# A hybrid encoder trunk: order of work by estimated times, and merged products in the units with stationary weights

## The chip, the cores and the metric

The kernel runs on one core of one Trainium2 chip. The metric is the device time of one execution in microseconds (us). PE is TensorE, PEld its weight loads, DVE VectorE, ACT ScalarE, POOL GpSimd and SP SyncE, which here only issues transfers.

## What is computed

Two layers work on 256 tokens of width 2048 (float32). Each normalises the stream, multiplies it by one wide input matrix, and feeds four branches: A, an S5 state-space layer (forward and backward scans, gelu, a gate product w_glu); B, a gated DeltaNet over six heads with a short convolution; C, grouped-query attention with eight heads; M, cross-attention into 256 memory tokens. Each branch result is multiplied by silu(z), lifted by its rows of w_branch, weighted by a sigmoid gate and summed; one output matrix and the residual end the layer. Cut to what matters:

```
h = rmsnorm(x) @ w_in            # u za | dq dk dv da db zb | aq ak av zc | mq zm | gate
yA, yB, yC, yM = s5(u), deltanet(dq, dk, dv, da, db), attention(aq, ak, av), memory(mq, mem)
merged = sum(sigmoid(gate_i) * ((y_i * silu(z_i)) @ w_branch_i) for i in "ABCM")
x = x + merged @ w_out
```

## The kernel before, in words

**The weight stream.** All weight matrices are packed into chunks of 128x1024 (512 KB). `layer_units` lists the units of a layer in the order of `ORDER`, and `layer` (from L1404) goes through them. `pump_raw` (L372) loads a chunk through SP's queue into one of three buffers. `pump_split` turns it into two parts, hi = rounded copy (ACT) and lo = raw - hi (DVE), each in three buffers; `hi` and `lo` are issued two chunks ahead (`AHEAD`). Activations (xT, memT, y, sy, mT) lie in two parts as well, side by side: `[128, 4, 2, 256]`.

**The products.** `run_unit` (its product is L418) multiplies a unit's chunks into one of two accumulators of two PSUM banks, `acc`. There are three kinds of units. N units (gates, branch and output products and some others) keep activations stationary and stream 512 weight columns. T units (u, km, mq, the DeltaNet projections dqkv, the four z and glu) and the one D unit per layer (dab) keep a tile of weights stationary and stream 256 tokens; a T unit of 16 row tiles has four chunks. Per weight tile there are three products: hi by activation hi, hi by activation lo, and, later in the chunk, lo by activation hi. All three go into columns 0 to 255 of a bank:

```
405  c = kk * u.cols
...
418  nc.tensor.matmul(o, w, x, start=start, stop=stop)
```

The line numbers are those of the profile. Line L240 is a helper through which all other instructions of PE, ACT and DVE are recorded, so these rows are told apart by their tiles: `bank` is one of four PSUM banks of the branches, `scr` one of 13 scratch tiles.

**Evacuation.** After a unit, `evac_<name>` reads `acc[:, :, 0:256]` (T) or all of it (N). For dqkv, ACT makes the centre tap of the convolution and DVE adds the four others, all from PSUM; for the z units, ACT takes tanh and DVE multiplies.

**The order around it.** Every branch is a set of generators, here called fibers. After every half chunk of products (6 or 12 matmuls) a tick passes. A fiber yields the number of ticks it wants to let pass; of those that are due, the one with the lowest rank goes on, as long as a count of issued work on DVE and ACT stays under a limit (`Meter`, `LIMIT`). S5 has rank 5, the last, in layer 0 and 3 in layer 1. All instructions thus stand in a fixed order on each engine's queue, written at build time; an instruction at the head of a queue that waits for a semaphore holds up those behind it.

```
while all(self.load[e] < self.LIMIT[e] for e in self.load):
    f = next((f for f in self.fibers if f[0] <= self.tick_no), None)
    if f is None:
        break
    self.rank = f[2]
    f[0] = self.tick_no + next(f[1])
```

**Steps that the prediction speaks of.** In S5, `chunk_sums` runs as three fibers over twelve blocks: two loads of 256 KB (L1253), 4 ticks, then TensorE multiplies the block directly (`bank<-scr,s5u`). `outputs` runs as two fibers: two loads of Wd (L1302, L1303) and two of Cd (L1305), 6 ticks, an addition on DVE and two copies on ACT, 2 ticks, the product, a copy, 2 ticks, a transposition, 1 tick, a copy. Then eight transfers write the result (L1338), one reads it back in another layout (L1343, `s5y`), and the gelu makes `sy`, the activations of glu. Before the first unit of each z the stream waits for the branch's result, before the products of M for attention's normed queries (`cqT`).

Of the kernel before, what the change touches and what calls it, by code (L numbers as in the profile page):

```python
# [2 lines left out]

# [10 lines left out]
AP = bass.AP  # L14
# [45 lines left out]
class Unit:  # L60
    def __init__(self, kind, name, src, nk, layer, idx=0, br=None):
        self.kind, self.name, self.src, self.nk = kind, name, src, nk
        self.layer, self.idx, self.br = layer, idx, br
# [11 lines left out]
def layer_units(layer):  # L75
    """The weight stream of one layer, in the order in which the tensor engine takes it."""
# [47 lines left out]
def dqkv_tile(j):  # L124
    """The j-th 128-column tile of the DeltaNet projections, head by head."""
# [4 lines left out]
def pack_weights(inp):  # L130
    """All weight matrices as the stream of [128, 1024] chunks that the kernel reads."""
# [23 lines left out]
def pack_small(inp):  # L155
    """Gains, biases and the like, per layer, one value or row per partition."""
# [20 lines left out]
def pack_s5(inp):  # L177
    """Per layer and partition (direction, state): a, log step, b and c; and d as diagonal blocks."""
# [12 lines left out]
def shape_consts():  # L191
    """Constants that follow from the shapes: identity, rotary angles, masks of the two directions."""
# [20 lines left out]
class Bank:  # L213
    """A set of equal tiles handed out and taken back in program order."""

    def __init__(self, tiles):
        self.free = list(tiles)

    def put(self, *tiles):
        self.free += tiles  # L220


class Meter:
# [5 lines left out]
    def __init__(self, eng, load, names, per, fixed):  # L229
        self._e, self._load, self._names, self._per, self._fixed = eng, load, names, per, fixed  # L230

    def __getattr__(self, name):
        f = getattr(self._e, name)

        def call(*args, **kw):
            o = kw.get("in_", kw.get("out", args[0] if args else None))
            if o is not None and name != "dma_start":
                for e in self._names:
                    self._load[e] += self._fixed + self._per * o.free_size()
            return f(*args, **kw)  # L240
        return call


class Builder:
    # microseconds of each engine per tick, and the backlogs between which the branches' work goes on
    DRAIN = {"V": 1.1, "S": 1}
    LIMIT = {"V": 2.125, "S": 2}
    FLOOR = {"V": 0.7, "S": 0.8}
    # memory attention, DeltaNet, attention and S5 by layer, and the preparation of S5
    RANK = ((3, 2, 4, 5), (5, 2, 4, 3))  # L250
    PREP_RANK = (3.5, 2.5)
    # ticks between the work of another engine and the tensor engine's use of it
# [3 lines left out]
    def __init__(self, ctx, tc, a, out):  # L256
        self.tc, self.nc, self.a, self.out = tc, tc.nc, a, out
        self.ready, self.count, self.acts = set(), {}, {}
        self.fibers, self.deferred, self.tick_no, self.rank = [], [], 0, 0
        self.load = {"V": 0.0, "S": 0.0}  # L260
        self.at = 0
        self.V = Meter(tc.nc.vector, self.load, "V", 1.04e-3, 0.06)
        self.S = Meter(tc.nc.scalar, self.load, "S", 0.84e-3, 0.19)
        self.PE = Meter(tc.nc.tensor, self.load, "VS", -0.6e-3, -0.02)
# [1362 lines left out]
```

## Time and profile before

| | |
|---|---|
| runs | 2330.08, 2333.71, 2336.09 us |
| median | 2333.71 us |
| profiled execution, span | 2329.0 us |
| mean granted TensorE clock | 0.990 of full speed |
| DMA | 523.39 MB, 225 GB/s on average |

The span is from the first to the last instruction of one profiled execution, whose own time as a run is not given beside it; the runs lie 1 to 7 us above it. Busy time on PE is an upper figure, since its products overlap in the rows.

### The profile page before, as it was taken

The numbers are of one execution on the slowest core, as the hardware profiler recorded it, in microseconds if no ns is written. First come the engines' busy times: TensorE is split into PE (matmuls) and PEld (weight loads), VectorE is DVE, ScalarE is ACT, GpSimd is POOL, SyncE is SP. The second block draws the span as 40 slices with busy tenths as digits, with TensorE's granted clock in tenths as the row PEclk, the third lists the DMA queues.
The fourth block names the chain that finished last, engine by engine and source line by source line (L and its number), as shares of the span: only waits on it lengthen the run. The fifth ranks groups of instructions, "written<-read, shape, count | busy, mean of one in ns | idle before, by whom it ended". The sixth has DMA issues, their size and how long they took to land.

```text
span 2329.0 us, 38887 instructions
## 1 busy us (share of the span) xinstructions
PE 2261.9 (97%) x14684; PEld 1960.0 (84%) x14684; DVE 1704.0 (73%) x2824; ACT 1245.9 (53%) x2176; POOL 88.3 (4%) x153
## 2 busy tenths in 40 slices
PE   6999999999999999799999999999999999999997
PEld 6888978988988788697789987889888878888886
DVE  6788878858768955689688856888547895566564
ACT  6655564565564355555655554665646445554443
POOL 0000000000010000000000001000000000000000
PEclk9999999999999999999999999999999999999999
DMA  6677678745776488678776795656468558877674
GB/s 222 226 240 249 213 248 276 228 153 182 212 241 194 145 305 303 185 246 276 250 239 197 237 302 178 223 180 198 157 194 271 186 175 283 286 230 245 231 239 146
DMA packets 245133, 523.39 MB, mean 225 GB/s; under 512 B 59320, under 2 KB 111032, under 8 KB 244304
## 3 DMA queue, kind: packets, MB, share of 16 engines
q1 hardware_dynamic: 218400, 471.41, 63.1%
q10 hardware_dynamic: 21952, 36.80, 4.4%
q0 software_dynamic: 4592, 12.69, 1.6%
q8 instruction: 115, 1.88, 0.3%
q14 instruction: 74, 0.61, 0.1%
HBM read 468.21 MB, written 65.18 MB: 229 GB/s over the span
## 4 chain that ended last, share of the span: by engine, by line
PE 87%; DVE 5%; DMA 3%; ACT 3%; issue 1%; SPq 0%; ACTq 0%; POOL 0%; POOLq 0%; DVEq 0%
PE acc L418 78%; PE bank L240 9%; DVE lo L240 2%; DMA raw<-wpack 2%; ACT hi L240 1%; DVE scr L240 1%; DVE dnx L240 1%; ACT scr L240 0%; DVE s5s L240 0%; DMA xm<-x 0%; DMA s5y<-Yd 0%; SPq L1243 0%; ACT gt L240 0%; DMA oTA<-gt 0%; DMA Rb<-Rd 0%
## 5 line engine op out<-in xcount | busy, mean ns | idle before, releaser
L240 DVE TENSOR_TENSOR lo<-raw,hi 128x1024 fp32r<-128x1024 f32 (+1 forms) x720 | 873.5, 1216 | 528.1 <-ACT hi L240 512.5
L240 ACT ACTIVATE hi<-raw 128x1024 fp32r<-128x1024 f32 (+1 forms) x720 | 757.7, 1055 | 712.8 <-PE acc L418 368.6
L418 PE MATMUL acc<-hi,xT 128*128 128x512 f32 x2432 | 633.5, 398 | 3.0 <-ACT hi L240 2.4
L418 PEld LDWEIGHTS acc<-hi,xT 128*128 128x128 f32 x2432 | 447.0, 189 | 98.6 <-issue 5.6
L418 PE MATMUL acc<-xT,hi 128*128 128x256 f32 x3392 | 460.6, 287 | 8.1 <-DVE xT L240 5.6
L418 PEld LDWEIGHTS acc<-xT,hi 128*128 128x128 f32 x3392 | 427.6, 193 | 20.2 <-issue 8.4
L418 PE MATMUL acc<-lo,xT 128*128 128x512 f32 x1216 | 327.3, 391 | 2.6 <-DVE lo L240 2.5
L418 PEld LDWEIGHTS acc<-lo,xT 128*128 128x128 f32 x1216 | 228.2, 188 | 54.1 <-DVE lo L240 4.8
L418 PE MATMUL acc<-xT,lo 128*128 128x256 f32 x1696 | 238.8, 284 | 0.0
L418 PEld LDWEIGHTS acc<-xT,lo 128*128 128x128 f32 x1696 | 219.4, 192 | 0.1
L240 ACT ACTIVATE scr<-bank 128x128 f32<-128x128 f32 (+6 forms) x324 | 105.2, 335 | 140.9 <-PE bank L240 111.0
L418 PE MATMUL acc<-hi,y 128*128 128x512 f32 x640 | 163.2, 395 | 0.0
L418 PEld LDWEIGHTS acc<-hi,y 128*128 128x128 f32 x640 | 117.6, 188 | 25.3 <-issue 1.0
L418 PE MATMUL acc<-hi,mT 128*128 128x512 f32 x512 | 131.3, 397 | 0.0
L240 DVE TENSOR_TENSOR dnx<-dnx 32x30 f32<-32x30 f32 (+9 forms) x360 | 114.6, 318 | 10.4 <-DVE dnx L240 0.5
L418 PEld LDWEIGHTS acc<-hi,mT 128*128 128x128 f32 x512 | 95.3, 190 | 19.5 <-issue 0.4
L418 PE MATMUL acc<-lo,y 128*128 128x512 f32 x320 | 85.8, 390 | 0.0
L240 DVE TENSOR_TENSOR scr<-scr,scr 128x512 f32<-128x512 f32 (+4 forms) x132 | 77.4, 590 | 3.6 <-DMA scr<-s 1.1
L240 DVE SCALAR_TENSOR_TENSOR hT<-acc,small,hT 128x254 f32<-128x254 f32 (+1 forms) x144 | 69.3, 481 | 3.9
L418 PEld LDWEIGHTS acc<-lo,y 128*128 128x128 f32 x320 | 60.1, 188 | 12.8
L418 PE MATMUL acc<-lo,mT 128*128 128x512 f32 x256 | 68.6, 390 | 0.0
L240 PE MATMUL bank<-consts,scr 128*128 128x128 f32 x388 | 62.3, 274 | 5.3 <-DVE memT L240 5.2
(186 smaller groups left out, 2036.8 us busy)
## 6 DMA issues: line engine op xcount, KB each, us to landing
raw<-wpack SPq DMA_DIRECT2D x714, 512.0 KB, 4.2
Bd<-scr ACTq DMA_DIRECT2D x48, 256.0 KB, 4.4
Cd<-scr SPq DMA_DIRECT2D x48, 256.0 KB, 4.6
Wd<-Kd SPq DMA_DIRECT2D x32, 384.0 KB, 6.8
scr<-Bd SPq DMA_DIRECT2D x48, 256.0 KB, 5.5
scr<-Wd SPq DMA_DIRECT2D x48, 256.0 KB, 4.9
scr<-Cd SPq DMA_DIRECT2D x48, 256.0 KB, 5.5
Rb<-Rd SPq DMA_DIRECT2D x48, 128.0 KB, 4.5
```

The lines of the kernel that those rows point to most:

```text
L240: return f(*args, **kw)
L418: nc.tensor.matmul(o, w, x, start=start, stop=stop)
```

## The change

**Products.** In T and D units the products of the weights' high part with both activation parts become one: the moving operand is the activations' two parts side by side, 512 columns, and the output is a whole bank. The product with the weights' low part goes into columns 256 to 511. The two halves are added in the evacuation (`fold`): ACT copies the second half out of PSUM, DVE adds the first. In dqkv the centre tap moves from ACT to DVE, and all taps read the folded copy.

**Order.** Ticks and `Meter` go. A `Clock` keeps an estimated time for each engine and for each piece of every tile (last write, last read), and every instruction, recorded through `Engine`, moves it on by an estimated duration. A fiber that yields goes on when the estimated end of what it has issued, plus 0.25 us, has passed on TensorE's estimated time; the number that it yields counts no more. Fibers of evacuation and of the loads of o and gates have rank -1, ahead of all others. A test comes after every three (N) or four (T, D) products. Weight loads are issued when the buffer's last reader is estimated to be done within 0.3 us; hi and lo of a chunk when their source is estimated to be there, at the latest one chunk ahead. Scratch tiles and banks are handed out by the time they come free. The waits for a branch's result (z units) and for `cqT` move from before the products into the evacuation.

The diff, cut to its core (removed comments and mere renamings left out):

```diff
+class Clock:
+    RING = {"raw": 3, "hi": 3, "lo": 3, "acc": 2}
...
+    def dma(self, eng, out, in_):
...
+        kb = max(out.size(), 1) * 4 / 1024
+        self.t[eng] = dep + (0.5 if eng == "G" else 0.06)
+        land = dep + 2.0 + kb / 200.0
+        self.mark(land, W, R)
...
+    def _time(self, op, outs, ins, kw):
+        n = outs[0].free_size()
+        if self._n == "PE":
+            if op == "transpose":
+                return 0.109
+            if ins[1].dtype == F32R:
+                return n / 2400 + 0.0133
+            rows, cols = ins[0].shape[0], ins[0].free_size()
+            share = max(0.25, cols / 128) * max(0.25, rows / 128)
+            return max(0.03, (4 * n / 2400 + 0.027) * share)
...
-    DRAIN = {"V": 1.1, "S": 1}
-    LIMIT = {"V": 2.125, "S": 2}
-    FLOOR = {"V": 0.7, "S": 0.8}
+    LIMIT = 2.0
+    LIMIT_EVAC = 4.0
+    MARGIN = 0.25
...
+    def tick(self):
+        self.pump_raw(self.ahead, False)
+        self.splits()
+        seen = set()
+        while True:
+            now, back = self.time(), self.backlog()
+            f = next((f for f in self.fibers if f not in seen and f.t + self.MARGIN <= now
+                      and back < (self.LIMIT_EVAC if f.rank < 0 else self.LIMIT)), None)
+            if f is None:
+                return
+            self.cur, self.rank, self.clock.end = f, max(f.rank, 0), 0.0
+            n = next(f.gen, "end")
+            f.busy = max(f.busy, self.clock.end)
...
+            elif n:
+                f.t, f.busy = max(f.t, f.busy), 0.0
...
-    def pump_raw(self, i):
+    def pump_raw(self, i, force=True):
         while self.next_raw <= min(i, len(self.queue) - 1):
+            old = self.next_raw - 3
+            if not force and (old in self.raw or self.gone.get(old, 0.0) > self.time() + 0.3):
+                return
...
+    def splits(self, upto=-1):
+        while self.pending:
+            n, e, w = self.pending[0]
+            r = self.raw[n]
+            src = r if e == "S" else self.split[n][0]
+            if n > upto and self.clock.written(src) > max(self.time(), self.clock.t[e]) + 0.1:
+                return
...
-                        o = acc[:, t, 0:256]
-                        hh, lh, hl = (hi[:, s], x[:, 0, :]), (hi[:, s], x[:, 1, :]), (lo[:, s], x[:, 0, :])
-                    todo += [(k, o, *hh, first, False), (k, o, *lh, False, False)]
+                        o = acc[:, t, 256:512]
+                        hl = (lo[:, s], x[:, 0, :])
+                    if u.kind == "N":
+                        todo += [(k, o, *hh, first, False), (k, o, *lh, False, False)]
+                    else:
+                        todo.append((k, acc[:, t, :].rearrange("p (i c) -> p i c", i=2), hi[:, s], x, first, False))
                     late.append((k, o, *hl, False, last))
...
+    def fold(self, out, acc, nt=2):
+        self.S.activation(out=out, in_=acc[:, 0:nt, 256:512], func=AF.Copy)
+        yield 1
+        self.V.tensor_tensor(out=out, in0=acc[:, 0:nt, 0:256], in1=out, op=ALU.add)
...
     def evac_dqkv(self, u, acc, l):
...
+        yield from self.fold(xs, acc)
         for x, c, s, w in tiles:
-            self.S.activation(out=c, in_=x, func=AF.Copy, scale=w[:, 2:3])
-        yield 1
-        for x, c, s, w in tiles:
+            V.tensor_scalar(out=c, in0=x, scalar1=w[:, 2:3], scalar2=None, op0=ALU.mult)
             for q in (0, 1, 3, 4):
...
         for u in self.units[l]:
...
-            if u.name == "prod" and u.br == "M":
-                self.need(("cqT", l))
...
-            if u.name[0] == "z" and u.idx == 0:
-                self.need((u.br, l))
...
+            if before is not None:
+                self.idle(lambda: before.emptied)
             self.need(key + (0,))
             acc = self.run_unit(u, self.acts[key])
-            f = getattr(self, "evac_" + u.name)
-            self.deferred.append((0, lambda f=f, u=u, acc=acc: f(u, acc, l)))
+            self.spawn(self.empty(u, acc, l, last), -1)
+            before, last = last, u
```

## Rows read from the trace of the kernel before

**Rows 1.** Head of the page and its section 1: busy time, share of the span, instructions.

```profile
span 2329.0 us, 38887 instructions
PE 2261.9 (97%) x14684; PEld 1960.0 (84%) x14684; DVE 1704.0 (73%) x2824; ACT 1245.9 (53%) x2176; POOL 88.3 (4%) x153
```

**Rows 2.** Two pieces of the chain that ended last: start, us, what, products.

```profile
1516.09 11.52 PE acc L418 x96
2234.68 80.27 PE acc L418 x354
```

**Rows 3.** Groups by form, TensorE's stream: count, then busy us, mean ns, idle before.

```profile
L418 PE MATMUL acc<-xT,hi 128*128 128x256 f32 x3392 | 460.6, 287 | 8.1 <-DVE xT L240 5.6 <-ACT hi L240 1.9 <-ACT gcol L240 0.5
L418 PE MATMUL acc<-xT,lo 128*128 128x256 f32 x1696 | 238.8, 284 | 0.0
L418 PE MATMUL acc<-memT,hi 128*128 128x256 f32 x256 | 34.3, 285 | 0.0
L418 PE MATMUL acc<-sy,hi 128*128 128x256 f32 x144 | 21.4, 301 | 10.4 <-ACT sy L240 9.7 <-DVE sy L240 0.6 <-ACT hi L240 0.2
```

**Rows 4.** Waits of TensorE's products (five of 14, and the last): total us, times, longest.

```profile
PE bank L240 <- ACT xm L240: 13.2, 1, 13.2
PE acc L418 <- ACT sy L240: 9.7, 1, 9.7
PE acc L418 <- DVE xT L240: 5.6, 3, 2.4
PE bank L240 <- DVE memT L240: 5.2, 2, 2.9
PE bank L240 <- DVE mT L240: 2.2, 1, 2.2
PE bank L240 <- DVE xm L240: 0.3, 1, 0.3
```

**Rows 5.** Groups by form: operations like those that the change adds or removes.

```profile
L240 ACT ACTIVATE pt<-bank 128x512 fp32r<-128x512 f32 x24 | 14.3, 596 | 11.3 <-PE bank L240 10.4 <-DVE lo L240 0.5 <-ACT scr L240 0.4
L240 DVE TENSOR_TENSOR pt<-bank,pt 128x512 fp32r<-128x512 f32 x24 | 16.4, 681 | 0.0
L240 ACT ACTIVATE hT<-acc,small 128x256 f32<-128x256 f32 x36 | 14.9, 464 | 0.0
L240 DVE TENSOR_SCALAR scr<-scr,dng 64x256 f32<-64x256 f32 x2 | 0.7, 346 | 0.1
```

**Rows 6.** Windows: busy us (instructions) of PE, PEld, DVE, ACT, POOL; PEclk; DMA; GB/s.

```profile
411.00:446.00 35.00, 35.00 (x294) 35.00 (x293) 32.19 (x60) 17.52 (x24) 0.52 (x1) 1.00 0.67 213
```

**Rows 7.** Timeline of S5's outputs in layer 0: SP, and TensorE's wait.

```profile
815.86 0.42 SPq L1302 DMA_DIRECT2D scr<-Wd  x1
...
911.97 0.43 SPq L1302 DMA_DIRECT2D scr<-Wd  x1
...
929.80 7.69 SPq L1338 DMA_DIRECT2D Yd<-s5o  x8
...
940.63 0.37 SPq L1343 DMA_DIRECT2D s5y<-Yd  x1
...
954.01 0.58 PE L418 MATMUL acc<-sy,hi 128*128 128x256 f32 x1 [9.66 <-ACT sy L240]
```

**Rows 8.** S5's loads by line: ns of one issue (min/median/max), time to landing.

```profile
L1253 SPq DMA_DIRECT2D scr<-Bd x48: 319/422/670, 621.4 to 1798.4; - x48
DMA to landing us min/median/max: 3.9/5.5/7.1
...
L1305 SPq DMA_DIRECT2D scr<-Cd x48: 320/423/1222, 816.8 to 2026.6; - x48
DMA to landing us min/median/max: 3.6/5.5/6.7
```

**Rows 9.** Waits of the SP queue: total us, times, longest.

```profile
SPq L372 <- DVE lo L240: 1197.7, 487, 8.0
```

**Rows 10.** Windows again: the stretch in which S5's outputs run.

```profile
815.00:930.00 115.00, 115.00 (x886) 97.58 (x885) 64.47 (x71) 60.98 (x101) 1.38 (x2) 1.00 0.89 305
```

More of the change, by code (lines that the diff above doesn't have):

```diff
@@ L213, with __init__ @@
 class Bank:
-    def __init__(self, tiles):
-        self.free = list(tiles)
+    def __init__(self, clock, tiles):
+        self.clock = clock
+        self.free = [(0.0, i, t) for i, t in enumerate(tiles)]
+        self.n = len(self.free)
     def put(self, *tiles):
[L220 to L233, printed above, removed]
-        def call(*args, **kw):
[L236 to L240, printed above, removed]
-        return call
+        for t in tiles:
+            self.n += 1
+            self.free.append((self.clock.last(t), self.n, t))
+        self.free.sort(key=lambda f: f[:2])
@@ L256, in __init__ @@
     def __init__(self, ctx, tc, a, out):
[L257 to L264, printed above, removed]
-        self.G = tc.nc.gpsimd
+        self.tc, self.a, self.out = tc, a, out
+        self.clock = Clock()
+        eng = lambda n, e: Engine(e, n, self.clock)
+        nc = tc.nc
+        self.V, self.S, self.PE, self.G, sp = (eng(n, e) for n, e in (("V", nc.vector), ("S", nc.scalar), ("PE", nc.tensor),
+                                                                     ("G", nc.gpsimd), ("SP", nc.sync)))
+        self.nc = SimpleNamespace(vector=self.V, scalar=self.S, tensor=self.PE, gpsimd=self.G, sync=sp)
+        self.ready, self.count, self.acts = {}, {}, {}
+        self.fibers, self.cur, self.pending, self.now = [], None, [], 0.0
+        self.rank, self.late, self.last, self.ahead = 0, {}, None, -1
         ep = lambda name, bufs=1, **kw: ctx.enter_context(tc.tile_pool(name=name, bufs=bufs, **kw))
@@ L301, in spawn, with time, mark @@
     def spawn(self, gen, rank=None):
-        self.fibers.append([self.tick_no, gen, self.rank if rank is None else rank])
-        self.fibers.sort(key=lambda f: f[2])
+        f = Fiber(gen, self.rank if rank is None else rank)
+        if self.cur:
+            f.t = max(self.clock.end, self.cur.busy)
+        self.fibers.append(f)
+        self.fibers.sort(key=lambda f: f.rank)
+    def time(self):
+        self.now = max(self.now, self.clock.t["PE"])
+        return self.now
+    def mark(self, key):
+        t = max(self.clock.end, self.cur.busy if self.cur else 0.0)
+        self.ready[key] = max(self.ready.get(key, 0.0), t)
@@ L306, in wait, with there @@
+    def there(self, key):
+        return key in self.ready and self.ready[key] + self.MARGIN <= self.time()
     def wait(self, key):
-        while key not in self.ready:
-            yield 1
+        while not self.there(key):
+            yield POLL
     def take(self, bank, n):
-        while len(bank.free) < n:
-            yield 1
-        out, bank.free = bank.free[:n], bank.free[n:]
-        return out
+        while True:
+            out = bank.take(n, self.time() + 0.3)
+            if out is not None:
+                return out
+            yield POLL
@@ L357, in stream_setup, with idle @@
+    def idle(self, test):
+        guard = 0
+        while not test():
+            self.tick()
+            if test():
+                break
+            self.now = self.time() + 0.25
+            guard += 1
+            assert guard < 20000, "never ready"
+    def need(self, key):
+        if not self.there(key):
+            self.idle(lambda: self.there(key))
     def stream_setup(self):
```

332 lines of the change are left out of this document (238 added, 94 removed).

## The prediction

> **What bounds the kernel now.** I read the page's busy line first. TensorE's products are busy 97% of a span of 2329.0 us, VectorE 73%, ScalarE 53% [rows 1]. Busy matmul rows overlap, so this alone proves no bound. The chain of work that ended last consists mostly of runs of products, and two of its pieces give a product's real price. In the last, 354 products of 512 columns follow each other in 80.27 us, 226.7 ns each; in one of 96 products of 256 columns, 11.52 us make 120.0 ns each [rows 2]. Half the columns therefore cost more than half the time: 2 x 120.0 - 226.7 = 13.3 ns.
>
> The table by form gives the counts. The units that keep weights stationary (kinds T and D) take three 256-column products per weight tile, of which the two with the weights' high part number 3392 + 256 + 144 = 3792; the remaining third of these units is 1896 products [rows 3]. At 120.0 ns the 5688 make 682.6 us. A unit with 512 weight columns has no product to merge.
>
> The waits list says how much TensorE loses to others. Its 14 rows sum to 52.5 us, of which 13.2 are the start, 9.7 the wait of the product w_glu for the S5 branch's result, 13.0 the transposed streams (xT 5.6, memT 5.2, mT 2.2), and small ones the rest [rows 4]. So the stream is bound by products. An ideal order could win at most 52.5 - 13.2 = 39.3 us; everything else must come from the products.
>
> **The change, part by part.** *Merged products.* Each pair (high weights by high activations, high weights by low) becomes one product of 512 columns into both halves of the bank. There are 3792 / 2 = 1896 pairs, and each saves 13.3 ns: 1896 x 13.3 = **25.3 us**, all on TensorE and so on the path. The operands are contiguous and the output fills one bank, as in the products that cost 226.7 ns, so I take the rows' price whole. The bounds are 0 and 25.3.
>
> The fixed part of a product, by the rows, is 120.0 - 256 / 2.4 = 13.3 ns. The Trainium skill (TensorE: Matmul & The Clock Gate, Back-to-back issue gap) puts it at about 2.5 ns, which would make this 4.7 us instead of 25.3. The rows measure both sizes in this kernel's own stream, and they decide.
>
> *The fold.* The halves must be added. Each of the 62 T units (31 per layer) gets a ScalarE copy and a VectorE add of 128x512 out of PSUM; the nearest rows are 0.596 and 0.681 us [rows 5]. That is 62 x 0.681 = 42.2 us for VectorE and 62 x 0.596 = 37.0 for ScalarE. In the DeltaNet projections the centre tap moves as well: 36 ScalarE operations of 0.464 us go (16.7 us), and 36 VectorE ones come; the form of the same width takes 0.346 [rows 5], 12.5 us in all. Together VectorE gets 55 us and reaches about 1759, 76% of the span. Both engines have room on average, so I cost this at nothing; what hides it is the next unit's products, since there are two accumulators. The cover is thinnest in the projections: from 411 to 446 us VectorE is already busy 32.19 of 35.00 [rows 6], and three units there add 3 x (0.68 + 2 x 0.35) = 4.1. That is 36.3 us of work in some 34. The surplus of 2 us in each of six such stretches goes into the units after it, since on average VectorE is idle for 27% of the time [rows 1]. Uncovered it would be 12 us.
>
> *The new order.* A step no longer waits for a fixed number of half chunks. It goes on when the planner's clock says that its own work has ended, plus 0.25 us; weight loads and their splits are issued when the clock says that buffer or data are there. Two waits of the stream move behind the products (the branch result of z, and the norm of attention's queries), where the accumulators cover them. What this can take away is in the waits list. S5's outputs are the clearest case: the twelve blocks' loads are issued between 815.86 and 911.97 us, 8.7 us apart, where each of two fibers passes 11 half chunks per block. What follows them is bound by data: the results leave at 929.80, the reload is issued at 940.63, and TensorE has stood 9.66 us when it begins at 954.01 [rows 7]. By the planner's clock a block's own steps take some 8 us per fiber (3.5 for the loads, then five short steps with 0.25 us and a test each), so the last block can come tens of us earlier, and this wait needs only 10. I count those 9.7 us as gone, and of the 13.0 us for the transposed streams 5, since these chains are as long as before and only their gaps shrink: -15. The bounds are 0 and -39.3.
>
> What it can add is the early use of loads. The planner puts a load of 256 KB at 2.0 + 256 / 200 = 3.3 us, and a consumer follows 3.5 us after the issue. The rows say otherwise: S5's input blocks land 3.9 us after issue at best and 5.5 in the median, and each issue takes SP 0.42 us, against 0.06 in the planner; the output blocks are alike, 3.6 and 5.5 [rows 8]. TensorE itself reads the input blocks (24 groups, two loads each). The tests come every three or four products, so on average 0.34 us is gained. With the median, a group waits 0.42 + 5.5 - 3.5 - 0.34 = 2.1 us, and 24 groups make 50; with the best, 0.5 us and 12. The output groups (24, four loads) put 0.68 us of VectorE work, 0.25 of margin and two ScalarE copies of 64x256 first, 0.45 each by the row of 128x256 [rows 5]: 1.27 + 5.5 - 3.5 - 0.34 - 1.8 = 1.1 us, or 27 in all, with the median, and nothing with the best. So the new waits lie between 0 (the old plan's list names no load that TensorE's products waited for [rows 4]) and 77 us. I take 14, near the best landing. At present the loads queue behind weight loads that SP holds for a free buffer (487 such waits, 1197.7 us [rows 9]); in the new order a weight load is issued only when its buffer is nearly free.
>
> The Trainium skill (DMA: Bandwidth & Descriptors, Anatomy of one DMA) fits 2.0 us plus the bytes at 436 GB/s, 2.6 us for such a load, by which the new waits would be none. The rows say 3.9 at the least.
>
> *Sum.* -25.3 - 15 + 14 = -26.3 us on a span of 2329.0: 2302.7. The three runs shown have a median of 2333.7, 4.7 above this span, so I forecast **2307 us**.
>
> **The rivals.** *More is won.* No load is late and most waits go: from -25.3 - 15 = -40.3 (2293 us) down to -25.3 - 39.3 = -64.6 (2269). For it: TensorE's waits are few and named. Against: start-up chains stay. The skill's price of a load, cited above, belongs here.
>
> *It is given back.* The late loads cost 33 to 47 us, which takes the other two terms away: 2327 to 2341.
>
> *Slower: S5's loads arrive late in front of TensorE.* Its queue is in order, so a product that waits for a block holds up the whole weight stream. The places are the two S5 stretches of each layer; from 815 to 930 the DMA engines are already 0.89 busy with 305 GB/s [rows 10]. Shorter gaps between the steps ask for the same bytes in less time, so landings grow rather than shrink. It decides where 48 groups lose over 0.98 us each on average (47 us). At the upper bound of 77 the sum is -25.3 - 15 + 77 = +37, 2370 us; with the first gain also lost, 2385. For it: both the landing and the issue rows are above the planner's figures. Against: S5 has the last rank in layer 0, so its steps often come later than the clock allows.
>
> *The merged product saves nothing.* If a product of 512 columns took twice 120.0 ns here, because the columns now come from two activation parts, the first term would be 0: -15 + 14 = -1 us, 2333. The price of 226.7 ns in the units with 512 weight columns speaks against it. The 2.5 ns of the skill's page would come close to this case, at 2328.
>
> **How the numbers follow.** What a measurement of this kernel can tell from no change is about 0.3%, 7 us. Chances: the forecast (2294 to 2326) 0.48, more won 0.13, given back 0.13, merged product saves nothing 0.03, slower (2341 to 2385) 0.23. Faster is 0.48 + 0.13 = 0.61, the same 0.16, slower 0.23. The range for 8 in 10 is 2272 to 2362: it takes in the forecast and the unchanged case, nearly all of "more won", and the slower case to its middle, which leaves about 0.13 outside. Cases of both signs are in it; the likeliest one's own range is 2294 to 2326.
>
> **What would show it.** In the profile after: 1896 products of 128x512 in T units and 1896 of 128x256, and a chain piece of the former at 227 ns each; VectorE near 1760 us and ScalarE near 1265. TensorE's wait for sy should be short, and waits for scr<-Bd and scr<-Cd (or for the sums of the latter) should total some 14 us. The forecast is wrong if these waits pass 40 us, if the weight stream's raw loads become what TensorE waits for, or if VectorE's lo parts come late in the projections.

## The result, and the profile after

The changed kernel took 2372.1 us (median of four runs) beside 2334.9 us for the kernel before: a ratio of 1.016, 95% interval [1.015, 1.018], so 37 us **slower**. The forecast was 2307 us with a range of 2272 to 2362. The profiled execution has a span of 2367.4 us, 38.4 more than before [rows 1]. Its page begins:

```profile
span 2367.4 us, 35196 instructions
...
PE 2262.0 (96%) x12788; PEld 1865.3 (79%) x12788; DVE 1757.0 (74%) x2930; ACT 1259.4 (53%) x2190; POOL 89.8 (4%) x153
```

1896 products fewer than before, and VectorE at 1757 us, ScalarE at 1259: the added and removed work is what the diff says. The groups by form (busy us, mean ns, idle before) show it one by one, to be read against [rows 3, 5]:

```profile
L361 PE MATMUL acc<-xT,hi 128*128 128x512 f32 x1696 | 437.5, 399 | 20.1 <-ACT hi L361 11.5 <-DVE xT L361 3.9 <-ACT xT L361 3.2
...
L361 DVE TENSOR_TENSOR gt<-acc,gt 128x512 f32<-128x512 f32 x56 | 38.3, 684 | 6.6 <-ACT gt L361 6.5
L361 ACT ACTIVATE gt<-acc 128x512 f32<-128x512 f32 x62 | 36.2, 583 | 6.8 <-PE acc L361 5.9 <-DVE ym L361 0.4 <-ACT scr L361 0.4
...
L361 PE MATMUL acc<-memT,hi 128*128 128x512 f32 x128 | 32.6, 396 | 0.0
...
L361 PE MATMUL acc<-sy,hi 128*128 128x512 f32 x72 | 18.7, 395 | 2.4 <-DVE scr L361 2.3
...
L361 DVE TENSOR_SCALAR hT<-gt,small 128x256 f32<-128x256 f32 x36 | 12.6, 350 | 0.6
```

1696 + 128 + 72 = 1896 merged products stand where 3792 stood. The fold's add takes 0.684 us, its copy 0.583, a centre tap 0.350, all close to the rows from which the prediction took them. A piece of the chain that ended last gives a unit's price (start, us, what, products):

```profile
1830.58 11.18 PE acc L361 x64
```

A unit of 96 products took 11.52 us [rows 2]; the same unit is now 32 merged products and 32 of 256 columns in 11.18 us. With 0.120 us for the latter, a merged product takes (11.18 - 32 x 0.120) / 32 = 229 ns, so a pair saves 240 - 229 = 10.6 ns instead of 13.3, and 1896 pairs 20 us. That gain is there; more than it was lost elsewhere. The waits of TensorE's products (total us, times, longest; 14 rows in all), beside [rows 4]:

```profile
PE bank L361 <- ACT scr L361: 28.0, 19, 3.2
PE acc L361 <- ACT hi L361: 17.7, 12, 5.9
PE bank L361 <- ACT xm L361: 13.4, 1, 13.4
PE bank L361 <- DVE scr L361: 8.1, 2, 6.7
PE bank L361 <- DMA scr<-Bd: 4.1, 6, 1.6
PE acc L361 <- DVE xT L361: 3.9, 2, 2.6
...
PE bank L361 <- DMA scr<-Cd: 0.2, 1, 0.2
```

The 14 rows sum to 90.4 us, against 52.5 before. The wait for sy (9.7 before) is gone. In its place stand small waits: 28.0 us of branch products for ScalarE's copies into scratch tiles, in 19 pieces, and 17.7 of the stream for hi. Of the 28.0, 19.4 us (ten pieces, seven in layer 0 and three in layer 1) stand in front of the products of S5's outputs; nearly all the rest is in DeltaNet and attention. The stretch of the outputs in layer 0 shows how they come about. First two windows (as in [rows 6, 10]; the upper one is the stretch of the projections, the lower one that of the outputs), then the timeline of SP, VectorE, ScalarE and TensorE:

```profile
411.00:446.00 35.00, 35.00 (x200) 30.72 (x199) 33.71 (x66) 15.42 (x19) 0.52 (x1) 1.00 0.62 194
823.00:877.00 54.00, 43.75 (x355) 32.53 (x355) 18.85 (x25) 24.88 (x57) 0.69 (x1) 0.87 0.89 311
```

```profile
602.49 3.65 SPq L361 DMA_DIRECT2D dnz<-Xd  x8
606.24 5.86 SPq L361 DMA_DIRECT2D s5u<-Ud  x8
612.20 9.55 SPq L361 DMA_DIRECT2D raw<-wpack  x4
...
823.33 0.90 SPq L361 DMA_DIRECT2D scr<-Wd  x2
...
830.42 0.65 PE L361 MATMUL bank<-scr,scr 128*32 128x128 f32 x16 [1.39 <-ACT scr L361]
...
833.44 0.65 PE L361 MATMUL bank<-scr,scr 128*32 128x128 f32 x16 [2.15 <-ACT scr L361]
...
834.82 1.91 PE L361 MATMUL acc<-lo,xT 128*128 128x512 f32 x4
...
848.31 1.10 SPq L361 DMA_DIRECT2D scr<-Wd  x2
...
853.13 0.69 DVE L361 TENSOR_TENSOR scr<-scr,scr 128x512 f32<-128x512 f32 x1 [4.33 <-DMA scr<-Wd]
...
853.86 0.84 ACT L361 ACTIVATE scr<-s5s 64x256 f32<-64x256 f32 x2 [4.50 <-DVE scr L361]
...
854.75 0.64 PE L361 MATMUL bank<-scr,scr 128*32 128x128 f32 x16 [2.16 <-ACT scr L361]
...
875.64 1.00 SPq L361 DMA_DIRECT2D scr<-Wd  x2
...
886.80 7.21 SPq L361 DMA_DIRECT2D Yd<-s5o  x8
...
902.09 0.38 SPq L361 DMA_DIRECT2D s5y<-Yd  x1
```

The twelve blocks are issued between 823.33 and 875.64, where the old order took 815.86 to 911.97 [rows 7]. At 853 us the chain is complete: VectorE stands 4.33 us for the table rows of Wd, ScalarE 4.50 for VectorE, and TensorE, with the weight stream queued behind the branch's products, 2.16 for ScalarE. VectorE's list has this wait 19 times:

```profile
DVE scr L361 <- DMA scr<-Wd: 42.4, 19, 4.3
```

The window shows two things more. TensorE is busy 43.75 of 54.00 us, and its granted clock is 0.87 there, while the old stretch had 1.00 [rows 10]: right after two waits of 1.4 and 2.2 us four products of 512 columns take 1.91 us, 0.48 each with their tail, about twice the 0.227 of the full clock; from 834.9 to 838.1 us the granted clock is 0.50, the lower of its two levels (1.2 GHz instead of 2.4). Over the whole span the clock is 0.985 against 0.990, by which 2367 x 0.015 - 2329 x 0.010 = 12 us are lost, an estimate.

The page splits the 38.4 us. TensorE's idle time, the span less its busy time, rose from 2329.0 - 2261.9 = 67.1 to 2367.4 - 2262.0 = 105.4 us, and the listed waits make 37.9 of these 38.3. Its busy time did not fall: the 20 us saved by merged products are used up inside it, by the estimated 12 us of lower clock and some 8 that no run here places.

The first three lines of the timeline above show another kind of loss. At 602 us SP issues eight loads for DeltaNet and eight of S5's input, 9.5 us in all; the weights follow at 612.20, and that makes the longest wait for hi (5.9 us at 620).

The same unit can be looked up in both traces by its first product: prod 3C of layer 0 begins 19.9 us later than before, zb 0 32.5, glu 0 only 15.8 (the wait for sy is gone), gate 2C of layer 1 41.9. Losses come in steps of 5 to 18 us, at the chunk sums and outputs of S5 and in attention, with a slow gain in between.

### The profile page after: what moved, and what is told of

Read it like the earlier page. It is cut to its first block, busy times and chain, and to the rows that moved or that the text cites. A ratio compares the mean times of both kernels' runs of the same rounds, so it can differ in the third digit from the quotient of the medians.

```text
span 2367.4 us, 35196 instructions
## 1 busy us (share of the span) xinstructions
PE 2262.0 (96%) x12788; PEld 1865.3 (79%) x12788; DVE 1757.0 (74%) x2930; ACT 1259.4 (53%) x2190; POOL 89.8 (4%) x153
## 4 chain that ended last, share of the span: by engine, by line
PE 58%; DMA 8%; DVE 6%; issue 3%; ACT 2%; SPq 1%; POOL 0%; ACTq 0%; DVEq 0%; POOLq 0%
PE acc L361 51%; PE bank L361 7%; DMA raw<-wpack 4%; DVE lo L361 3%; SPq L361 1%; ACT hi L361 1%; DMA scr<-Bd 1%; DVE scr L361 1%; DMA scr<-Wd 1%; ACT scr L361 1%; DVE dnx L361 1%; DMA scr<-Cd 1%; DMA Ud<-gt 1%; DMA oTB<-scr 0%; DVE hT L361 0%
## 5 line engine op out<-in xcount | busy, mean ns | idle before, releaser
L361 PEld LDWEIGHTS acc<-hi,xT 128*128 128x128 f32 x2432 | 453.1, 190 | 100.5 <-ACT hi L361 5.3
L361 PE MATMUL acc<-xT,hi 128*128 128x512 f32 x1696 | 437.5, 399 | 20.1 <-ACT hi L361 11.5
L361 PEld LDWEIGHTS acc<-xT,hi 128*128 128x128 f32 x1696 | 306.6, 191 | 80.8 <-ACT hi L361 13.4
L361 PE MATMUL acc<-lo,xT 128*128 128x512 f32 x1216 | 344.8, 400 | 0.0
L361 PEld LDWEIGHTS acc<-xT,lo 128*128 128x128 f32 x1696 | 231.5, 191 | 21.3 <-issue 3.1
L361 PE MATMUL acc<-xT,lo 128*128 128x256 f32 x1696 | 243.8, 285 | 1.5 <-DVE lo L361 1.4
L361 DVE TENSOR_TENSOR scr<-scr,scr 128x512 f32<-128x512 f32 (+4 forms) x132 | 77.5, 591 | 44.7 <-DMA scr<-Wd 42.4
L361 DVE SCALAR_TENSOR_TENSOR hT<-gt,small,hT 128x254 f32<-128x254 f32 (+1 forms) x144 | 69.7, 484 | 5.1
L361 ACT ACTIVATE gt<-acc 128x512 f32<-128x512 f32 (+1 forms) x94 | 68.6, 729 | 6.9 <-PE acc L361 5.9
```

The source lines that it names most:

```text
L361: o = f(*args, **kw)
```

## The experiments

Ratios are to the kernel before on the same chip; 0.001 is 2.3 us. Each kernel is built from the one before or after by the edit shown, cut to its core.

### The three parts apart

*The new order with three products* (fold kept):

```diff
-todo.append((k, acc[:, t, :].rearrange("p (i c) -> p i c", i=2), hi[:, s], x, first, False))
+todo += [(k, acc[:, t, 0:256], hi[:, s], x[:, 0, :], first, False),
+         (k, o, hi[:, s], x[:, 1, :], False, False)]
```

> The new order with three products per pair again (hi by hi into columns 0 to 256 of the half bank pair, the other two into 256 to 512, so that the fold stays). The changed kernel measured 2372.1 us. Theory: the merged product saves what the sum said, 62 units of 0.35 to 0.41 us, also inside the new order, so this run takes 2372 + 22 to 25 = 2394 to 2397 us, and the whole loss lies in the order. Rival, the merged product saves nothing because TensorE waits elsewhere for the same work: 2369 to 2376 us. Rival, the faster TensorE is what makes the loads late: under 2369 us.

Measured 1.0228 [1.0206, 1.0251], 2384.5 us. Against the change's 1.0162 the merged product is worth 0.0066, 15 us, with some 6 us of uncertainty by the two intervals: between two of the cases, and not clearly less than the 20 us that the unit's rows give.

*The old order with merged products and fold* (new products and evacuations; ticks stay, the first in each chunk of a T unit now after 6 products instead of 12):

```diff
-todo += [(k, o, *hh, first, False), (k, o, *lh, False, False)]
+todo.append((k, acc[:, t, :].rearrange("p (i c) -> p i c", i=2), hi[:, s], x, first, False))
...
+yield from self.fold(s, acc)
```

> The kernel before, in its own order by ticks, with only the merged product and the fold of its two halves. Theory: 62 units of 0.35 to 0.41 us come off and the fold lies beside TensorE, so 2308 to 2314 us, faster than both kernels. Rival, the fold's extra work on ScalarE and VectorE meets the stretches where VectorE is full (92% in one of them) and gives half of it back: 2318 to 2327 us. Rival, the faster units make the loads late in this order too: over 2330 us.

Measured 1.0277 [1.0258, 1.0296], 2392.6 us: slower than the change itself. The theory was that the products alone are a gain; it fell. The time is in the last rival's range, but the next run shows the loss without faster units.

*The old order with the fold alone* (the same, three products into the two halves):

> The kernel before with three products per pair as before, but the first into columns 0 to 256 of its half and the other two into 256 to 512, so that the fold and its additional work on ScalarE and VectorE stand alone; the merged product is not there. The merged product with the fold, in the same order by ticks, took 1.028 of the kernel before (64 us more), where its saving alone would have been 22 to 25 us less. Theory: the fold is what costs, since VectorE is full in the stretch of the DeltaNet projections and S5's chain and the convolutions queue behind each other there, so 2365 to 2400 us. Rival, what costs is that a tick of 12 products turned into one of fewer columns while the branches count ticks: the fold by itself is hidden, 2325 to 2336 us.

Measured 1.0330 [1.0310, 1.0350], 2407.8 us. This is on the theory's side, 8 us above its range, and more than all of the fold's work on VectorE: the fold costs 77 us, where VectorE's busy time rises by 56 (1759.6 us). Merging the products then wins 12 back.

*The new order alone* (evacuations and products of before, no fold):

```diff
-o = acc[:, t, 256:512]
+o = acc[:, t, 0:256]
...
-yield from self.fold(xs, acc)
```

> The changed kernel's order by estimated times with the products and the evacuations of the kernel before: three products per pair into the same 256 columns, no fold. With the fold and three products the same order took 1.0228 of the kernel before (53 us more). Theory: the order alone is the loss, since its loads are planned to land before they do; the fold is hidden, so 2370 to 2386 us. Rival, the fold holds most of it: 2325 to 2345 us. Rival, both halve it: 2346 to 2369 us.

Measured 1.0095 [1.0078, 1.0112], 2353.7 us, the third case. All corners together:

| order | products per pair | fold | ratio |
|---|---|---|---|
| by ticks | two | no | 1 |
| by ticks | two | yes | 1.0330 |
| by ticks | merged | yes | 1.0277 |
| by estimated times | two | no | 1.0095 |
| by estimated times | two | yes | 1.0228 |
| by estimated times | merged | yes | 1.0162 (the change) |

Along the change's own path: order +22 us, fold +31, merged products -15, together 38. By the other path it is fold +77, merged products -12, order -27: once the fold is in, the new order is the faster of the two. The parts do not simply add up; what one costs depends on what is there already.

### Why the fold costs so much

Its work, or something else? Two kernels take it apart in the order by ticks, where I expected nothing else to move. One adds VectorE work that nobody waits for:

```diff
+def extra(self, *ws):
+    for w in ws or (384, 128):
+        x = self.idle_work[:, 0:w]
+        self.V.tensor_tensor(out=x, in0=x, in1=x, op=ALU.add)
```

> The kernel before, with VectorE work added at the places of the fold that nobody waits for: in each T unit two additions on a spare tile (384 and 128 columns in the place of the fold's 512) and in the projections two more of 256 in the place of the centre taps, some 53 us of VectorE time in all. Products and evacuations are those of the kernel before. Theory A (VectorE's time where it is full): most of the fold's 77 us, 1.017 to 1.035, 2370 to 2412 us. Theory B (the longer chain): 0.998 to 1.006, 2326 to 2345 us.

Measured 1.0318 [1.0289, 1.0347]. In the other ScalarE copies the accumulator, there is nothing to add, and the evacuation goes on from the copy a tick later:

```diff
+self.S.activation(out=out, in_=acc[:, 0:nt, 0:256], func=AF.Copy)
+yield 1
```

> The kernel before, with the chain of the fold but without its work on VectorE: ScalarE copies each T and D unit's accumulator first (all three products in the same 256 columns, so there is nothing to add), and the evacuation goes on one tick later from the copy; the centre tap stays on ScalarE. Theory A (VectorE's time): 0.998 to 1.008, 2326 to 2349 us. Theory B (the longer chain, and ScalarE's 37 us): 1.017 to 1.035, 2370 to 2412 us.

Measured 1.0213 [1.0196, 1.0230]. Each lies in the range of another theory, A the first and B the second, and together they would make more than the fold has. What the two kernels share is that `Meter` counts the added work, and the count decides when a branch goes on. So the next pair parts work and count. Work without the count, all other instructions at their old places:

```diff
-        self.V.tensor_tensor(out=x, in0=x, in1=x, op=ALU.add)
+        self.nc.vector.tensor_tensor(out=x, in0=x, in1=x, op=ALU.add)
```

> The kernel before with the same 53 us of VectorE work that nobody waits for, but not counted: every other instruction keeps its place in its engine's queue. Counted, this work took 1.032. Theory A (VectorE's time where it is full): 1.015 to 1.032, 2364 to 2403 us. Theory C (the loss is the new arrangement, since the old one was tuned with its counts): 1.000 to 1.008, 2329 to 2347 us.

Measured 1.0063 [1.0045, 1.0080], 2343.2 us. And the count without the work:

```diff
-        self.V.tensor_tensor(out=x, in0=x, in1=x, op=ALU.add)
+        self.load["V"] += 0.06 + 1.04e-3 * w
```

> The kernel before with the same amounts added to the count of VectorE's issued work, and no instruction added: only the order of the branches' work changes. Theory A (VectorE's time): 0.998 to 1.008, 2324 to 2347 us. Theory C (the arrangement): 1.015 to 1.032, 2364 to 2403 us.

Measured 1.0268 [1.0251, 1.0285], 2390.9 us: **63 us slower without one instruction more** on VectorE but the memset of the spare tile. Both are what the theory of the arrangement expected. The work itself costs 15 us. The trace of the kernel with uncounted work shows that the work was there and where it went: its page, the window of the projections [rows 6], and two of its waits:

```profile
span 2336.7 us, 39043 instructions
...
PE 2265.0 (97%) x14684; PEld 1960.9 (84%) x14684; DVE 1762.1 (75%) x2987; ACT 1245.5 (53%) x2176; POOL 88.5 (4%) x153
```

```profile
411.00:446.00 35.00, 35.00 (x286) 34.66 (x285) 33.85 (x68) 16.50 (x24) 0.52 (x1) 1.00 0.56 192
```

```profile
PE acc L420 <- ACT sy L240: 9.5, 1, 9.5
PE acc L420 <- ACT hi L240: 7.7, 8, 1.6
```

VectorE has 58 us more, is busy 33.85 of 35.00 us in that stretch, and TensorE still loses nothing there; the wait for sy is that of before (9.7), the one for hi is longer (4.5 before). Now the kernel with the count alone, its page, its waits and its timeline on VectorE and TensorE:

```profile
PE 2275.0 (95%) x14684; PEld 1967.8 (82%) x14684; DVE 1706.2 (71%) x2825; ACT 1245.7 (52%) x2176; POOL 89.2 (4%) x153
```

```profile
PE acc L420 <- ACT sy L240: 17.0, 1, 17.0
...
PE bank L240 <- DVE ckv L240: 10.6, 1, 10.6
PE bank L240 <- DVE pt L240: 9.2, 1, 9.2
```

```profile
635.05 0.28 PE L240 MATMUL bank<-pt,ckv 128*128 128x256 f32 x1
636.12 3.98 DVE L240 SCALAR_TENSOR_TENSOR hT<-acc,small,hT 128x254 f32<-128x254 f32 x8 [1.57 <-ACT hT L240]
...
641.25 2.62 DVE L240 TENSOR_TENSOR dnx<-dnx 32x130 f32<-32x130 f32 x10
643.79 0.67 DVE L240 TENSOR_TENSOR pt<-bank,pt 128x512 fp32r<-128x512 f32 x1
644.52 1.44 PE L240 MATMUL bank<-pt,ckv 128*128 128x256 f32 x5 [9.20 <-DVE pt L240]
```

The last split of attention's probabilities (pt) in layer 0 runs at 643.79 us. In the kernel before and in the one with uncounted work it ran here:

```profile
606.20 0.68 DVE L240 TENSOR_TENSOR pt<-bank,pt 128x512 fp32r<-128x512 f32 x1
...
609.18 0.68 DVE L240 TENSOR_TENSOR pt<-bank,pt 128x512 fp32r<-128x512 f32 x1
```

The fuller count held this last step back (the two splits ahead of it came earlier than before). It was issued only where the z units of branch C need the result and no product is issued in between, and there it stands behind eight taps and ten small operations on VectorE. TensorE waits 9.2 us. The kernel with the fold alone has this same wait (11.4 us), as has the one with counted work (12.2). So in the order by ticks a changed order without work costs 63 us, and work in an unchanged order 15. That most of the fold's own 77 us is of the first kind fits both and the shared wait, but is not shown by itself: the added work had no one waiting for it, and the fold with its copy was not run uncounted.

### The loads

*Landing and issue as measured, in the whole planner:*

```diff
-self.t[eng] = dep + (0.5 if eng == "G" else 0.06)
-land = dep + 2.0 + kb / 200.0
+self.t[eng] = dep + (0.5 if eng == "G" else 0.43)
+land = dep + (2.0 if out.tensor.name.startswith("raw") else 4.6) + kb / 200.0
```

> The changed kernel with one price of its planner altered: a load takes 4.6 us plus its bytes to land instead of 2.0 (weight loads keep 2.0), and its issue holds SyncE or ScalarE for 0.43 us instead of 0.06. Theory (loads planned too early; 28 and 18 us are lost in the two stretches of S5's outputs, 14 and 12 in those of its chunk sums): most of that comes back, 2310 to 2335 us, and VectorE's 44.7 us of idle time in front of the additions with the table rows falls under 10. Rival, VectorE's additional folds or the order of the other branches set the loss: 2362 to 2376 us with that idle time gone all the same.

Measured 1.0174 [1.0157, 1.0192], 2370.3 us: nothing gained, though VectorE's wait for Wd fell from 42.4 to 12.7 us. The time is the rival's, whose cause this run does not test. The plan moved. The timeline on TensorE near 905 us shows outputs back to back with no weight products between them, in a window with a granted clock of 0.63:

```profile
890.00:912.00 22.00, 10.81 (x136) 6.03 (x134) 4.39 (x9) 10.29 (x34) 1.79 (x2) 0.63 0.84 292
```

```profile
904.38 1.08 PE L361 MATMUL bank<-scr,scr 128*32 128x128 f32 x16 [1.42 <-ACT scr L361]
...
907.98 1.08 PE L361 MATMUL bank<-scr,scr 128*32 128x128 f32 x16 [1.22 <-ACT scr L361]
...
912.09 3.33 PE L361 MATMUL acc<-xT,hi 128*128 128x512 f32 x7 [1.67 <-DVE gt L361]
```

From 876 to 912 us only DeltaNet and S5's outputs run: zb 2 of layer 0 begins 51 us after zb 1 there, against 11 us in the changed kernel. By the code, zb 2 needs the accumulator of zb 0, whose evacuation now waits for DeltaNet's result.

*S5's outputs 3 us later, nothing else:*

```diff
     nc.sync.dma_start(out=ct[i], in_=self.Cd[b][:, i])
+self.clock.end += 3.0
 yield 6
```

> The changed kernel with 3.0 us more put between the issue of the loads of one block of S5's outputs and their use, nothing else. Theory: of the 38 us lost, the two stretches of the outputs hold 28 and 18 before other stretches give some back, so 2326 to 2350 us. Rival, the branch then ends later and the product on its gelu waits (9.7 us in the kernel before) take the gain: 2352 to 2366 us. Rival, the loads are late because the queue carries more in this order, whatever the pause: 2366 to 2378 us.

Measured 1.0062 [1.0045, 1.0079], 2343.9 us, in the theory's range: 23 us come off. The waits in the outputs' chain shrink (from 28.0 and 42.4):

```profile
PE bank L361 <- ACT scr L361: 13.9, 15, 3.0
...
DVE scr L361 <- DMA scr<-Wd: 9.9, 7, 3.1
```

Of the 13.9 us, 2.9 still stand in front of the outputs' products, where it was 19.4.

*The same pause in the new order without fold and merge:*

> The order by estimated times with the products and evacuations of the kernel before (1.0095 of it by itself), and S5's outputs 3 us later. Theory: what the order alone loses is the early use of the loads of S5's outputs (15 us in each layer are lost around them there), so 0.997 to 1.003, about 2323 to 2337 us. Rival, it loses in the attention branches and the chunk sums as well: 1.005 to 1.009, 2342 to 2351 us.

Measured 1.0053 [1.0036, 1.0071], 2341.7 us, against 1.0095: 10 us, at the lower end of the rival's range. Half of what the order alone loses is elsewhere. The rival's places are not confirmed: in layer 0 the largest step is at the fourth to sixth projection (gate 0M begins 25 us later than in the kernel before, zm 1, four units earlier, does not), and a good part of it is won back later.

*On top of the pause: the small loads through GpSimd, or the chunk sums later as well.*

```diff
-nc.sync.dma_start(out=T1[i][32 * q:32 * q + 32, :, 32 * q:32 * q + 32],
+nc.gpsimd.dma_start(out=T1[i][32 * q:32 * q + 32, :, 32 * q:32 * q + 32],
...
-nc.sync.dma_start(out=ut[16 * j:16 * j + 16], ...)
+nc.gpsimd.dma_start(out=ut[16 * j:16 * j + 16], ...)
```

> The kernel with S5's outputs 3 us later (1.0062 of the kernel before), and in addition the eight loads of S5's input and the eight of DeltaNet's triangular blocks issued by GpSimd, so that SyncE is not held for 4 to 9 us in front of the weight loads. Theory (SyncE's queue delays the weights; waits of TensorE on hi sum 14.6 us there): 8 to 15 us less, 2328 to 2336 us. Rival, the transfers themselves are slow and the weights were not what came last: 2338 to 2348 us. Rival, GpSimd's loads land so late that the chunk sums start late: over 2350 us.

```diff
     nc.sync.dma_start(out=W[hf], in_=self.Bd[b][:, hf])
+self.clock.end += 3.0
 yield 4
```

> The kernel with S5's outputs 3 us later (1.0062 of the kernel before), and in addition 3.0 us between the loads and the use of S5's chunk sums. Theory (in that kernel the chunk sums still lose 10 to 15 us in each layer to loads that come late): 12 to 25 us less, 2318 to 2332 us, faster than the kernel before or level with it. Rival, the loss there is the issue of small loads on SyncE in front of the weights, which a pause does not move: 2338 to 2348 us. Rival, the branch then ends later and the glu waits: 2348 to 2360 us.

Measured 1.0045 [1.0030, 1.0060] and 1.0050 [1.0034, 1.0065]; the kernel without them had 1.0062. Both intervals overlap with its own, so neither shows a gain by itself; the times, 2341.3 and 2342.1 us, lie in the range of the first rival of each.

### The projections

*Old order, merged except the 18 units of the DeltaNet projections:*

```diff
-if u.kind == "N":
+if u.kind == "N" or u.name == "dqkv":
     todo += [(k, o, *hh, first, False), (k, o, *lh, False, False)]
```

> The order by ticks of the kernel before, with merged products and fold in all T and D units except the 18 of the DeltaNet projections, which keep three products, no fold, and their centre tap on ScalarE. With them the same order took 1.028 of the kernel before. Theory: the fold costs where VectorE is full, and that is in the projections (each brings 0.67 us of fold and two centre taps of 0.35 us in front of what others wait for), so here nearly all of it is gone and the saving of 44 units stays, 44 x 0.25 to 0.4 = 11 to 18 us: 0.992 to 0.995, about 2312 to 2320 us, faster than both kernels. Rival, the fold costs as a longer chain in every unit (z, mq, km, glu): still 1.010 to 1.020, 2354 to 2377 us. Rival, the shorter ticks of merged units cost: 1.000 to 1.008.

Measured 1.0162 [1.0149, 1.0176]; with the projections merged it was 1.0277. So leaving out the projections gives back 27 us, but with the 44 other units merged 38 are still lost. That is the first rival's number; the runs on count and work offer another reason than a longer chain, but neither was tested on this kernel.

*New order, outputs later, the same exception:*

> The order by estimated times with S5's outputs 3 us later (1.0062 of the kernel before with everything merged), and the 18 units of the DeltaNet projections with three products, no fold, and their centre tap on ScalarE. The other 44 units stay merged. Theory: the projections' fold on a full VectorE still holds part of the loss in this order (the fold cost 31 us in it with three products), so 15 to 25 us come off and 4 to 7 us of saved products are lost: 0.996 to 1.001, about 2320 to 2332 us. Rival, in this order the fold is not what costs once S5's loads have time: 1.006 to 1.010, 2344 to 2354 us.

Measured 0.9997 [0.9985, 1.0009], 2329.8 us, in the theory's range and level with the kernel before; 15 us less than with the projections merged.

*Outputs later, all merged, the centre tap back on ScalarE:*

```diff
+yield 1
 for x, c, s, w in tiles:
-    V.tensor_scalar(out=c, in0=x, scalar1=w[:, 2:3], scalar2=None, op0=ALU.mult)
+    self.S.activation(out=c, in_=x, func=AF.Copy, scale=w[:, 2:3])
+yield 1
```

> The order by estimated times with S5's outputs 3 us later and everything merged (1.0062 of the kernel before); only the centre tap of the projections' convolution goes back from VectorE to ScalarE, reading the folded copy. 36 x 0.35 = 12.5 us leave VectorE, and each projection's evacuation gets one step more. Theory (what the projections' fold costs is VectorE's time where it is full): 36 of the taps and 18 of the folds make 12.5 + 12.1 us, which cost 15 + 4 to 7 us there, so half of it, 9 to 11 us, comes off: 1.001 to 1.003, 2332 to 2337 us. Rival (it is the longer chain): 1.006 to 1.010, 2343 to 2353 us.

Measured 1.0109 [1.0091, 1.0127], slower by 11 us than with the tap on VectorE. The rival comes nearest, but the trace does not show its longer chain as such: in layer 0 the unit after the projections (gate 0M) begins 15 us later, by waits like this one of a DeltaNet head, which the new plan put there:

```profile
457.39 0.46 PE L361 MATMUL bank<-scr,UA 32*32 32x32 f32 x16 [6.26 <-ACT scr L361]
```

A small edit plans everything after it anew. How much of this run, and of the 15 us above, is the edit itself and how much a lucky or unlucky plan stays open.

*With the small loads and the chunk sums moved, without and with the projections' fold:*

> The order by estimated times with S5's outputs 3 us later and the projections unmerged (0.9997 of the kernel before), and in addition the small loads issued by GpSimd and the chunk sums 3 us later, which took 0.0017 and 0.0012 off by themselves where the projections were merged. Theory: both act on the stretch in which that kernel still loses 18 us (the last projections and first chunk sums of layer 0: its window shows SyncE issuing ten loads of sums and four of inputs in front of the weights), so they add up or more: 0.990 to 0.997, about 2306 to 2322 us, faster than both kernels. Rival, the stretch is bound by the branches' own chain: 0.998 to 1.002.

> Everything merged, S5's outputs 3 us later, the centre tap back on ScalarE, and the small loads issued by GpSimd and the chunk sums 3 us later. Theory (VectorE's time in the projections, and loads, each holds its share): 0.996 to 1.000, 2320 to 2330 us. Rival (the chain behind each unit): 1.003 to 1.008, 2337 to 2348 us.

The first took **0.9976 [0.9967, 0.9986], 2324.7 us**, faster than both kernels, between its two cases: against 2329.8 us, the small loads and the sums are worth 5 us here. The second took 1.0071 [1.0053, 1.0088], the rival's range, and 9 us less than the centre tap alone. In the faster one TensorE's waits for ScalarE's copies into scratch tiles are down to 6.5 us (28.0 in the changed kernel).

## Why the prediction was wrong

**The merged products: right, a fifth too large.** 25.3 us were forecast. A unit's rows give 20, and the runs 15 in the new order and 12 in the old one, each with some 6 us of uncertainty; whether part of it is waited away again they do not settle. The Trainium skill (TensorE: Matmul & The Clock Gate, Back-to-back issue gap) gives about 2.5 ns as the gap of an isolated product and says that in a stream with weight loads both operations set the spacing. Its 2.5 ns would make this term an estimated 4.7 us; this stream, with one weight load for each product [rows 1], gives 20.

**The fold: this step failed.** It was costed at nothing, on the ground that both engines have room on average and the next unit's products hide it; 12 us if uncovered. By itself the fold costs 77 us in the old order and 31 in the new one. As work, the bound was near: 15 us for 58 us on VectorE, in the old order. But the sum took the queues of before as given and asked only whether the work fits beside them. In this kernel the instructions' order is computed from a count or a clock of issued work, and each added instruction enters it; a fuller count alone costs 63 us. The rows cited (VectorE 92% busy in the projections [rows 6]) were the wrong place to look: that stretch bore the uncounted work without a wait.

For the new order, the one that the change has, no run parts work from place, so how its 31 us divide stays open. Its waits speak for both engines' time as well: with the fold, TensorE's waits for hi go from 8.1 to 19.1 us, for lo from 1.7 to 6.9, and 8.3 for `gt`, the folded copy, are new.

**The new order: its gain right, its loss too small.** -15 + 14 were forecast, and the order alone costs 22. The gain came: the wait for sy went (9.7 us), the waits for xT, memT and mT fell from 13.0 to 9.0, and S5's outputs ended earlier. The loads came late, as forecast, but mostly by the way of Wd, VectorE and ScalarE. Bd and Cd land near the medians of before [rows 8], Wd later than its 4.9 us there:

```profile
scr<-Wd SPq DMA_DIRECT2D x48, 256.0 KB, 4.9
```

```profile
scr<-Bd SPq DMA_DIRECT2D x48, 256.0 KB, 5.6
scr<-Wd SPq DMA_DIRECT2D x48, 256.0 KB, 5.7
scr<-Cd SPq DMA_DIRECT2D x48, 256.0 KB, 5.8
```

The value of 14 was taken near the best landing, for both kinds of blocks together. For the outputs the median was the right one: it gave 27 us, their products wait 19.4, and the pause gives back 23. For the input blocks, which TensorE reads directly, even the sum by the best landing gave too much: 12 us, where the waits for Bd sum to 4.1. Together with 0.2 for Cd, 23.7 us stand against the 14, under the 40 that the text set as its sign of being wrong. So this term was 10 us short, and most of the rest of the order's cost was in no term: with the pause, the order alone still costs 12 us. The Trainium skill's fit for a load (DMA: Bandwidth & Descriptors, Anatomy of one DMA), made on GpSimd's path, gives an estimated 2.6 us for 256 KB, by which there would have been no wait at all; these loads go through SyncE, and the rows, 5.6 to 5.8 us, differ.

The deeper error is the view that the new order could lose at most the late loads. That takes the old order as one of many equals. Adding to its count alone, and thereby moving it, costs 63 us, the added copy 50, the planner by itself 22: each of these moves away from it was slower. Nothing in the rows read from its profile shows that; it takes a run.

**Not priced:** the clock. In the stretch shown, products after short waits ran at the lower clock; over the kernel this is an estimated 12 us, more than half of what the merged products save.

**The rivals.** The time, 2372, lies in the slower rival's range, and its mechanism (S5's loads in front of TensorE) was at work. That it is near the 2370 of that rival's sum is luck: the sum has 77 us of late loads, the trace 23.7, and the fold's 31 us, which no rival named, make up most of the difference.

## What to carry to other kernels

Where an edit changes the input of whatever generates the order, price the new order apart from the new work: add the work uncounted, and the count without work, and compare. The plan by estimated times needed slack where a load feeds a chain of three engines in front of the bound one; three microseconds in that one place were worth 23 us, the measured landing times everywhere nothing. And a saving on the bound engine is not yet a gain if another engine gets work for it: of the kernels tried, only the one with the projections left as they were, the loads spaced and the small ones moved off SyncE beats the old order, by 0.24%.

## What was not expected of the hardware

- After two waits of 1.4 and 2.2 us TensorE's granted clock stood at 0.50 from 834.9 to 838.1 us (four products of 512 columns took 1.91 us there), so these waits cost more than their own length.
- Eight loads of small pieces hold SyncE for 3.65 us (dnz) and 5.86 us (s5u), and weight loads wait behind them; issued by GpSimd they raised its busy time from 90 to 127 us (outputs 3 us later, without and with this), and TensorE's list of waits names none of these transfers.
- A merged product, its 512 moving columns from two activation parts, costs 229 ns beside the 226.7 of a product with 512 weight columns [rows 2].
